# Up stage of an expert layer: slot choosing over 46 blocks, modulation with a row in PSUM, rows turned later, and 24 modulation chunks moved over from the down stage

## Chip, cores and metric

The kernel runs on one core of one Trainium2 chip. The metric is the device time of one execution in microseconds (us), lower is better. All times below are of the kernel before the change, which was executed three times for the metric and once more under the profiler.

## What is computed

Two blocks of a network follow each other on 256 tokens of width 1024. The first block ends in a layer with 16384 experts, each a row of two tables:

```python
s1 = jnp.einsum('thd,hkd->thk', q[..., :half], keys1)
s2 = jnp.einsum('thd,hkd->thk', q[..., half:], keys2)
v1, i1 = lax.top_k(s1, PEER_TOPK)
v2, i2 = lax.top_k(s2, PEER_TOPK)
...
sv, pos = lax.top_k(cand, PEER_TOPK)
eidx = jnp.take_along_axis(cidx, pos, axis=-1)
gw = jax.nn.softmax(sv, axis=-1)
...
act = jnp.einsum('td,thkd->thk', xc, u)
hact = jax.nn.gelu(act) * gc
return jnp.einsum('thk,thkd->td', hact, jnp.take(v_tab, ec, axis=0))
```

The kernel does not gather. It multiplies the tokens with all 128 x 128 rows of the table `peer_u`, takes the gelu, multiplies with a dense matrix of gates that is zero wherever an expert was not chosen, and multiplies with all of `peer_v`. The second block needs a modulation beside it: a row silu(c) of 1024 numbers times a matrix `ada_w_2` of 1024 x 6144 for each of two layers, and for two of these six parts of layer 0 a second row, silu(c of the context), as well.

## The kernel before

**The two stages.** The up stage (`u_blocks`) walks over 128 blocks of 128 experts. For one block SP (the queue of SyncE) loads 512 KB of `peer_u`; ScalarE (ACT) rounds it to a high part (`u_split`, line L1042); GpSimd (POOL) subtracts to get the low part (L1043); TensorE (PE) does 24 matmuls of 128 x 256, three products for each of eight pieces (`mm3`, L227 to L229); ACT takes the gelu into the tile A (L1055). The split of block b+2 is issued before the matmuls of block b. The down stage (`v_blocks`) walks the same way over 128 blocks of `peer_v`: ACT L1063 and VectorE (DVE) L1064 split the table, DVE L222 splits the gated activations, and PE adds up with matmuls of 128 x 512 (L308, L309, L312).

**What is laid between.** Generators give out other work, one step at a time, between the blocks (`even` shares n steps over so many blocks):

- `topk` (58 steps) chooses the experts: on DVE the maxima and their indices, then comparisons and sums that turn positions into numbers (L974 to L980), a softmax with an Exp on ACT (L983), and at the end six PE transposes (L992), copied to the PSUM tiles `picks` (L994).
- `gates` (32 steps) makes the dense gates from the picks: three DVE comparisons and products of 128 x 1024 (L1012 to L1014), eight PE matmuls of 128 x 128 into two PSUM tiles `pg` (L1019), for each of these one DVE product into A (L1021) and one ACT copy (L1023) that goes to memory (`gate_scratch`). `late_gates` reads this back in the down stage and multiplies it into the other half of A (L1033).
- `ada` (one step a chunk) makes the modulation. A chunk is 128 rows of `ada_w_2`, loaded by SP (512 KB, L171) into one of three tiles; DVE multiplies it with the row and sums along it (scalar_tensor_tensor, L180, called an STT below); a chunk with two destinations takes two. After eight chunks DVE adds the bias (L186) and `to_row` turns the result into a row: a PE transpose (L193), a DVE copy (L195) and an SP store (L196).

In the up stage `topk` runs over blocks 0 to 72, `ada0` (24 chunks, of which the first 16 have two destinations) over blocks 0 to 99, `gates` over blocks 76 to 125. In the down stage `ada1` has 72 chunks, 40 over blocks 0 to 63 and 32 over 56 blocks of the second half.

**The order.** Each engine runs its own instructions in a fixed order, which a scheduler makes from the program; an instruction waits for the ones on other engines that it needs, and everything behind it on its engine waits too. SP issues all of these loads from one queue in order.

**Memory.** The row silu(c) (`ar[:, 3]`) and the second row (`ar[:, 4]`) lie in SBUF, copied to all 128 partitions, so both inputs of an STT come from SBUF. PSUM has a pool with the tags `mm` (2 tiles), `tr` (2) and `acc` (4). `near`, `picks` and half of the `pg` tiles are `acc`.

Of the kernel before, what the change touches and what calls it, by code (L numbers as in the profile page):

```python
# [17 lines left out]
D = 1024  # L18
# [66 lines left out]
def program(tc, I, out, C, taps=None, upto=99):  # L85
# [23 lines left out]
    def ps_mm(shape=(128, 256)):  # L109
        mm_tags[1] += 1  # L110
        tag = mm_tags[0][mm_tags[1] % len(mm_tags[0])]
        return psp.tile(list(shape), F32, name=tag, bufs=4 if tag == "acc" else 2)

# [3 lines left out]
    def ps_acc(shape=(128, 512)):  # L117
        return psp.tile(list(shape), F32, name="acc", bufs=4)

# [40 lines left out]
    def ada(chunks, cs, raws, junk=None):  # L160


        todo = [(l, j, c) for l, j, _ in chunks for c in range(8)]
        got = []

        def load():
            if todo:
                l, j, c = todo.pop(0)
                raw = raws[len(got) % len(raws)]
                with tc.issue_after(last_unit[0].ins):  # L170
                    Q.dma_start(raw, I["ada_w_2"][l, (8 * j + c) * 128:(8 * j + c + 1) * 128])  # L171
                got.append(raw)

        for _ in raws:
            load()
        n = 0
# [711 lines left out]
    big = b2.enter_context(tc.tile_pool(name="big", bufs=1, reuse_waits="tile"))  # L888
    wrk.pool = b2.enter_context(tc.tile_pool(name="wrk2", bufs=2, reuse_waits="tile"))
    half0 = ExitStack()  # L890
    A = [half0.enter_context(tc.tile_pool(name="half0", bufs=1, side="right", reuse_waits="tile")), big]
# [15 lines left out]
    for c in range(16):  # L907
# [10 lines left out]
        V.tensor_copy(sc[:, :, c], pt.rearrange("p (t k) -> p t k", t=2))  # L918
    tap("sc", sc)

    wk = keep.tile([128, 2 * D], F32, name="C8")
# [4 lines left out]

    picks = []

    def topk():
        sels = [flat(b, 1).rearrange("p (s c) -> p s c", s=2) for b in (99, 103)]  # L930
        gw = flat(101, 1).rearrange("p (t h k) -> p t h k", t=2, h=8)
        near = ps_acc()
        v1 = near[:, 0:128].rearrange("p (h k) -> p h k", h=8)
# [53 lines left out]
        V.tensor_tensor(gw, gw, r8.unsqueeze(3).to_broadcast([128, 2, 8, 16]), op=OP.mult)  # L987
        picks.extend([ps_acc().rearrange("p (j t) -> p j t", j=2), ps_acc((128, T))])
        for tt in range(2):
# [8 lines left out]
    g1d = nc.dram_tensor("gate_scratch", (32, 128, 2, 256), F32, kind="Internal").ap()  # L998
    ww = itertools.cycle([("wwh", ps_tr), ("wwl", ps_acc)])

# [3 lines left out]
    def gates():  # L1004


        pick, weight = picks
        io = iota.unsqueeze(1).to_broadcast([128, 8, 128])
        for n in range(32):
            ts = slice(8 * n, 8 * n + 8)  # L1010
            oa, ob = next(oas), next(obs)
            V.tensor_tensor(oa, io, pick[:, 1, ts].unsqueeze(2).to_broadcast([128, 8, 128]), op=OP.is_equal)  # L1012
            V.tensor_tensor(ob, io, pick[:, 0, ts].unsqueeze(2).to_broadcast([128, 8, 128]), op=OP.is_equal)
            V.tensor_tensor(ob, ob, weight[:, ts].unsqueeze(2).to_broadcast([128, 8, 128]), op=OP.mult)  # L1014
            for q in range(2):
# [6 lines left out]
                st = ww_tile(name, F32R).bitcast(F32)  # L1022
# [65 lines left out]
    ut, vt = {b: u_split(b) for b in range(2)}, {}  # L1088
    ar = flat(108, 20).rearrange("p (n d) -> p n d", n=5)
    for w in range(2):  # L1090
        row(ar[:, 3 + w], f"c{w}")
    ada0 = ada([(0, j, [(j, 0)] + [(12 + j, 1)] * (j < 2)) for j in range(3)], lambda w: ar[:, 3 + w],
               [ar[:, n] for n in range(3)], flat(104, 4))
    ADA, TOPK = 24, 58

# [4 lines left out]

    tk = topk()
    for i, _ in enumerate(u_blocks(0, 76)):
        even(tk, i, TOPK, 73)
        even(ada0, i, ADA, 100)
    for _ in tk:
        pass
    g0 = gates()
    for i, _ in enumerate(u_blocks(76, 128)):
        even(g0, i, 32, 50)
        even(ada0, i + 76, ADA, 100)  # L1110
        if i + 76 == 101:
            for _ in ada0:
                pass
    for _ in g0:
        pass
# [6 lines left out]
    at = xp.tile([128, 4, D], F32, name="xdt")  # L1122
    at = [at[:, n] for n in range(4)]
    row(at[3], "c0")
    ada1 = ada([(0, j, [(j, 0)]) for j in range(3, 6)] + [(1, j, [(6 + j, 0)]) for j in range(6)], lambda w: at[3], at[:3])
# [592 lines left out]
    right.close()  # L1718
    b3.close()
    top.close()  # L1720

# [17 lines left out]
```

## Time and profile before

| what | value |
|---|---|
| median of three runs | 2160.7 us (2158.08 to 2161.99) |
| the profiled execution | 2161.18 us |
| its span in the trace | 2159.4 us |
| PE busy | 2058.1 us, 95% of the span |
| DVE busy | 1607.4 us, 74% |
| ACT busy | 1030.4 us, 48% |
| POOL busy | 795.1 us, 37% |
| moved by DMA | 403.56 MB, 187 GB/s on average |

The up stage lies between about 519 and 979 us, the down stage between there and about 1358 us. PE is busy in nearly all of the span, so a change can only save what PE loses: stretches in which it stands still, and stretches in which it runs at a lower clock. The profile gives the granted clock of a stretch as a share (1.00 is the full 2.4 GHz, and between 1.00 and 0.50 it is a mix of 2.4 and 1.2 GHz). Busy time is told for each engine apart, so the rows of a stretch must be read beside each other: which engine is full there, and for whom PE waits.

### The profile page before, as it was taken

The page shows a single profiled execution, that of the slowest core. Times are in us where ns is not written, and L with a number is a line of the kernel's source. Part 1 is how long each engine was busy: PE and PEld are TensorE (multiplying, and loading weights), DVE is VectorE, ACT ScalarE, POOL GpSimd, SP SyncE. Part 2 cuts the span into 40 slices and gives each one's busy share as a digit, 9 for nine tenths or more (in the row PEclk, how much of TensorE's full clock was granted, in tenths as well). Part 3 has the DMA queues.
Part 4 walks back from the last instruction along what each step waited for, and adds up shares of the span by engine and source line. Part 5 has one row for each costly group of instructions (what it writes and reads, how often), then busy time and mean ns, then how long its engine had stood idle before and what let it go on. Part 6 is the DMA issues. An engine that isn't in the chain of part 4 may idle for free.

```text
span 2159.4 us, 37426 instructions
## 1 busy us (share of the span) xinstructions
PE 2058.1 (95%) x14726; PEld 1898.8 (88%) x14726; DVE 1607.4 (74%) x2576; ACT 1030.4 (48%) x1732; POOL 795.1 (37%) x392
## 2 busy tenths in 40 slices
PE   8999999999879999999999999999888999899999
PEld 7989999889879999997777777899876999798998
DVE  6677688779999346758997787536785877777877
ACT  5655565454434444444444555435524545445454
POOL 2221333113957876550000000323441556343554
PEclk9999999999989999999999999999999999899999
DMA  6544544456645766559998888746224655554552
GB/s 218 159 127 135 169 128 128 133 201 200 220 138 189 231 211 189 173 174 328 349 331 318 314 280 256 166 97 76 89 69 141 194 199 181 181 171 144 193 182 98
DMA packets 122035, 403.56 MB, mean 187 GB/s; under 512 B 14561, under 2 KB 23793, under 8 KB 121858
## 3 DMA queue, kind: packets, MB, share of 16 engines
q1 hardware_dynamic: 110688, 388.43, 54.4%
q0 software_dynamic: 1520, 3.75, 2.7%
q10 hardware_dynamic: 9650, 8.99, 1.2%
q8 instruction: 115, 1.88, 0.4%
q14 instruction: 62, 0.51, 0.1%
HBM read 390.56 MB, written 10.55 MB: 186 GB/s over the span
## 4 chain that ended last, share of the span: by engine, by line
PE 68%; DVE 17%; DMA 8%; issue 3%; ACT 3%; POOL 0%; SPq 0%; DVEq 0%; ACTq 0%; POOLq 0%
PE mm L227 15%; PE mm L228 14%; PE mm L229 14%; PE acc L309 4%; PE acc L312 4%; PE acc L308 4%; DMA xdt<-in_ada_w 3%; DMA wraw<-in_peer_v 3%; DVE A L180 3%; DVE wlo L1064 3%; PE tr L1019 1%; PE acc L1019 1%; DVE wlox L222 1%; DVE wlo L222 1%; ACT whi L1063 1%
## 5 line engine op out<-in xcount | busy, mean ns | idle before, releaser
L1043 POOL TENSOR_TENSOR wlo<-wraw,whi 128x1024 fp32r<-128x1024 f32 x126 | 321.3, 2555 | 182.6 <-ACT whi L1042 182.4
L227 PE MATMUL mm<-xdt,whi 128*128 128x256 f32 x1248 | 360.7, 290 | 7.1 <-ACT A L1055 5.7
L229 PE MATMUL mm<-xdt,wlo 128*128 128x256 f32 x1248 | 355.0, 285 | 0.6 <-POOL wlo L1043 0.6
L228 PE MATMUL mm<-xdt,whi 128*128 128x256 f32 x1152 | 327.9, 285 | 0.2 <-DVE xdt L418 0.2
L1042 ACT ACTIVATE whi<-wraw 128x1024 fp32r<-128x1024 f32 x128 | 135.7, 1060 | 236.0 <-PE mm L228 152.2
L227 PEld LDWEIGHTS mm<-xdt,whi 128*128 128x128 f32 x1248 | 240.5, 193 | 8.6 <-ACT A L1055 6.3
L229 PEld LDWEIGHTS mm<-xdt,wlo 128*128 128x128 f32 x1248 | 241.0, 193 | 1.4 <-POOL wlo L1043 1.2
L228 PEld LDWEIGHTS mm<-xdt,whi 128*128 128x128 f32 x1152 | 223.1, 194 | 0.4 <-DVE xdt L418 0.4
L222 POOL TENSOR_TENSOR wlo<-wraw,whi 128x1024 fp32r<-128x1024 f32 x37 | 93.8, 2538 | 308.4 <-ACT whi L217 271.6
L1063 ACT ACTIVATE whi<-wraw 128x1024 fp32r<-128x1024 f32 x128 | 134.6, 1057 | 106.8 <-DMA wraw<-in_peer_v 100.5
L1064 DVE TENSOR_TENSOR wlo<-wraw,whi 128x1024 fp32r<-128x1024 f32 x128 | 155.5, 1220 | 23.1 <-ACT whi L1063 22.9
L222 DVE TENSOR_TENSOR wlo<-wraw,whi 128x1024 fp32r<-128x1024 f32 x87 | 134.9, 1551 | 46.7 <-ACT whi L217 46.3
L227 PE MATMUL mm<-F,whix 128*128 128x256 f32 x560 | 158.6, 284 | 7.1 <-ACT whix L217 5.0
L217 ACT ACTIVATE whi<-wraw 128x1024 fp32r<-128x1024 f32 x124 | 130.7, 1055 | 71.9 <-PE mm L228 42.4
L228 PE MATMUL mm<-F,whix 128*128 128x256 f32 x560 | 158.5, 283 | 0.4 <-DVE F L418 0.4
L229 PE MATMUL mm<-F,wlox 128*128 128x256 f32 x560 | 158.2, 283 | 0.5 <-DVE wlox L222 0.5
L309 PE MATMUL acc<-wlo,wwh 128*128 128x512 f32 x512 | 149.9, 395 | 6.6 <-DVE wlo L1064 6.4
L312 PE MATMUL acc<-whi,wwl 128*128 128x512 f32 x512 | 147.2, 394 | 5.6 <-DVE wwl L222 5.4
L308 PE MATMUL acc<-whi,wwh 128*128 128x512 f32 x512 | 141.5, 393 | 5.5 <-ACT whi L1063 5.2
L275 POOL TENSOR_TENSOR wrawx<-wrawx,grow 128x1024 f32<-128x1024 f32 x38 | 107.0, 2828 | 90.5 <-DMA wrawx<-in_ffn_w_down 47.0
L1382 POOL MEMSET att<- 128x256 f32 x4 | 1.2, 312 | 358.2 <-DVE xdt L180 358.2
L309 PEld LDWEIGHTS acc<-wlo,wwh 128*128 128x128 f32 x512 | 95.5, 189 | 32.3 <-DVE wlo L1064 12.6
(619 smaller groups left out, 6321.6 us busy)
## 6 DMA issues: line engine op xcount, KB each, us to landing
wraw<-in_peer_u SPq DMA_DIRECT2D x128, 512.0 KB
wraw<-in_peer_v SPq DMA_DIRECT2D x128, 512.0 KB
xdt<-in_ada_w SPq DMA_DIRECT2D x72, 512.0 KB
wraw<-in_ffn_w_up SPq DMA_DIRECT2D x56, 512.0 KB
wraw<-in_w_in SPq DMA_DIRECT2D x42, 512.0 KB
wrawx<-in_ffn_w_up SPq DMA_DIRECT2D x32, 512.0 KB
wrawx<-in_ffn_w_down SPq DMA_DIRECT2D x31, 512.0 KB
wrawx<-in_w_in SPq DMA_DIRECT2D x30, 512.0 KB
```

Of the source, the lines that this page charges most:

```text
L217: S.activation(hi, raw, AF.Copy)
L222: eng.tensor_tensor(lo, raw, hi.bitcast(F32), op=OP.subtract)
L227: P.matmul(ps, ah, bh, start=start, stop=False)
L228: P.matmul(ps, ah, bl, start=False, stop=False)
L229: P.matmul(ps, al, bh, start=False, stop=stop)
L308: P.matmul(acc[tt][hf], ah, hi[:, fs], start=st_, stop=False, skip_group_check=free)
L309: P.matmul(acc[tt][hf], ah, lo[:, fs], start=False, stop=False, skip_group_check=free)
L312: P.matmul(acc[tt][hf], al, hi[:, fs], start=False, stop=sp_ and not free, skip_group_check=free)
L1042: S.activation(hi, raw, AF.Copy)
L1043: (G if b in POOL_U else V).tensor_tensor(lo, raw, hi.bitcast(F32), op=OP.subtract)
L1063: last_hi[0] = S.activation(hi, raw, AF.Copy)
L1064: V.tensor_tensor(lo, raw, hi.bitcast(F32), op=OP.subtract)
```

## The change

The up stage now shares its work out in another way, and the down stage has less of it.

1. `topk` is given out over blocks 0 to 45 (before 0 to 72).
2. `ada0` comes after it: 14 chunks over blocks 46 to 63, 34 over blocks 64 to 123. It has 48 chunks in place of 24 (all of layer 0); `ada1` has 48 in place of 72, of which 18 (before 40) stand in the down stage's first half and 30 (before 32) in its second.
3. `gates` is given out over blocks 64 to 123.
4. The row silu(c) is copied into a PSUM tile `c0` of two banks by two ACT copies; `near` and `weight` get a bank each. These four banks are the ones of the `acc` tiles, whose pool is closed for the up stage and opened again after it. The second row stays in SBUF. All `pg` tiles now have the tag `tr` with two buffers.
5. `to_row` is no longer done right after the bias is added but in the middle of the next eight chunks, or at the end.
6. The chunks have three tiles of their own (`adp`) in both stages, and the program's `dynamic_dma_scratch_size` is set to 4096.

```diff
+                if c == 4:
+                    while late:
+                        slot = late.pop(0)
+                        to_row(slot, mods[:, slot])
             for slot, w in dests:
                 V.tensor_tensor(mods[:, slot], mods[:, slot], col(f"ab{l}{j}", 0, 8), op=OP.add)
-                to_row(slot, mods[:, slot])
+                late.append(slot)
+        for slot in late:
+            to_row(slot, mods[:, slot])
...
+    sums[1].close()
+    sums[1] = ExitStack()
+    sums[0] = sums[1].enter_context(tc.tile_pool(name="row", bufs=1, space=bass.MemoryType.PSUM))
+    c0 = sums[0].tile([128, D], F32, name="c0")
+    near = sums[0].tile([128, 512], F32, name="near")
+    picks = [near.rearrange("p (j t) -> p j t", j=2), sums[0].tile([128, T], F32, name="weight")]
...
-                name, pool = next(ww)
-                pg = pool((128, 512)).rearrange("p (t i) -> p t i", t=4)
+                pg = ps_tr((128, 512)).rearrange("p (t i) -> p t i", t=4)
...
+    for hf in range(2):
+        S.activation(c0[:, FS[hf]], cr[:, 0, FS[hf]], AF.Copy)
+    chunks = ([(0, j, [(j, 0)] + [(12 + j, 1)] * (j < 2)) for j in range(6)] + [(1, j, [(6 + j, 0)]) for j in range(6)])
+    raws = [adp.tile([128, D], F32, name=f"ada{n}") for n in range(3)]
+    ada0 = ada(chunks[:6], lambda w: cr[:, 1] if w else c0, raws, flat(104, 4))
...
-    for i, _ in enumerate(u_blocks(0, 76)):
-        even(tk, i, TOPK, 73)
-        even(ada0, i, ADA, 100)
...
-    for i, _ in enumerate(u_blocks(76, 128)):
-        even(g0, i, 32, 50)
-        even(ada0, i + 76, ADA, 100)
...
+    for i, _ in enumerate(u_blocks(0, 128)):
+        if i < 46:
+            even(tk, i, 58, 46)
+        elif i < 64:
+            even(ada0, i - 46, 14, 18)
+        else:
+            even(g0, i - 64, 32, 60)
+            even(ada0, i - 64, 34, 60)
...
-        even(ada1, i, 40, 64)
+        even(ada1, i, 18, 64)
...
-        even(ada1, i, 32, 56)
+        even(ada1, i, 30, 56)
```

In the changed kernel the lines have moved: L171 is L178, L180 is L187, L186 is L197, L193 is L206, L195 is L208, L196 is L209, L200 is L213, L227 to L229 are L240 to L242, L249 is L262, L974 to L980 are L991 to L997, L992 is L1008, L994 is L1010, L1012 to L1014 are L1028 to L1030, L1019 is L1034, L1043 is L1058. Three places show how the order changes.

PE before, inside u block 23: the transpose of the first modulation row (L193) stands among the block's matmuls (mm).

```order
L228 MATMUL mm<-xdt,whi 128x256
L229 MATMUL mm<-xdt,wlo 128x256
L193 MATMUL tr<-ident,mods 8x128
L227 MATMUL mm<-xdt,whi 128x256
L228 MATMUL mm<-xdt,whi 128x256
```

PE in the changed kernel, inside u block 55: the same transpose (now L206, among L240 to L242).

```order
L240 MATMUL mm<-xdt,whi 128x256
L241 MATMUL mm<-xdt,whi 128x256
L206 MATMUL tr<-ident,mods 8x128
L242 MATMUL mm<-xdt,wlo 128x256
L240 MATMUL mm<-xdt,whi 128x256
```

The transpose has moved back by 32 u blocks.

DVE before, around the bias of the first row (L186): the STTs (L180) stand between the steps of the choosing (L974, L978, L980).

```order
L974 TENSOR_TENSOR A_5787<-acc,iota 128x1024
L180 SCALAR_TENSOR_TENSOR A_5787,mods<-A_5787 128x1024
L980 TENSOR_REDUCE A_5787<-A_5787 128x64
L978 TENSOR_TENSOR A_5787<-A_5787,acc 128x1024
L180 SCALAR_TENSOR_TENSOR A_5787,mods<-A_5787 128x1024
L186 TENSOR_TENSOR mods<-mods,cols 128x8
```

DVE in the changed kernel, from the last step of the choosing on (`near` and `weight` are PSUM tiles, c_6370 the row in PSUM, ada_ the chunk's tile, A_5793 a scratch tile and, as an input of a chunk's second STT, the second row).

```order
L997 TENSOR_REDUCE A_5793<-A_5793 128x64
L1010 COPY near<-tr 128x2x128 x2
L1028 TENSOR_TENSOR C_6373<-iota,near 128x1024
L1029 TENSOR_TENSOR C_6373<-iota,near 128x1024
L1028 TENSOR_TENSOR oa<-iota,near 128x1024
L1029 TENSOR_TENSOR ob<-iota,near 128x1024
L1030 TENSOR_TENSOR C_6373<-C_6373,weight 128x1024
L1030 TENSOR_TENSOR ob<-ob,weight 128x1024
L187 SCALAR_TENSOR_TENSOR A_5793,mods<-ada_6394,c_6370 128x1024
L187 SCALAR_TENSOR_TENSOR ada_6394,mods<-ada_6394,A_5793 128x1024
L187 SCALAR_TENSOR_TENSOR A_5793,mods<-ada_6395,c_6370 128x1024
L187 SCALAR_TENSOR_TENSOR ada_6395,mods<-ada_6395,A_5793 128x1024
```

All STTs now stand behind the choosing and behind the first gates' comparisons.

SP before, the loads of `peer_u` and of the chunks:

```order
L249 DMA wraw<-in_peer_u 128x1024 x7
L171 DMA A_5787<-in_ada_w 128x1024 x3
L249 DMA wraw<-in_peer_u 128x1024 x2
L171 DMA A_5787<-in_ada_w 128x1024
L249 DMA wraw<-in_peer_u 128x1024 x2
L171 DMA A_5787<-in_ada_w 128x1024
L249 DMA wraw<-in_peer_u 128x1024 x4
```

and in the changed kernel (row_c is the second row, read into its tile):

```order
L262 DMA wraw<-in_peer_u 128x1024 x6
L213 DMA A_5793<-row_c 128x1024
L262 DMA wraw<-in_peer_u 128x1024 x44
L178 DMA ada_6394<-in_ada_w 128x1024
L178 DMA ada_6395<-in_ada_w 128x1024
L178 DMA ada_6396<-in_ada_w 128x1024
L262 DMA wraw<-in_peer_u 128x1024 x2
L178 DMA ada_6394<-in_ada_w 128x1024
L262 DMA wraw<-in_peer_u 128x1024
L178 DMA ada_6395<-in_ada_w 128x1024
L178 DMA ada_6396<-in_ada_w 128x1024
```

The first three chunks have moved from behind the 7th load of `peer_u` to behind the 50th, and from there on chunks and `peer_u` loads take turns nearly one to one.

## Rows read from the trace of the kernel before

**Rows 1.** Windows: us, busy of PE, PEld, DVE, ACT, POOL, clock, DMA share, GB/s

```profile
518.00:979.00 461.00, 436.16 (x3605) 432.90 (x3604) 329.13 (x545) 198.60 (x329) 321.32 (x126) 0.97 0.60 194
...
700.00:800.00 100.00, 100.00 (x842) 100.00 (x841) 43.18 (x47) 45.84 (x76) 77.79 (x32) 1.00 0.68 223
```

**Rows 2.** Waits of PE in the up stage: total us, times, longest

```profile
PE tr L193 <- DVE mods L186: 18.1, 1, 18.1
PE mm L227 <- ACT A L1055: 5.7, 3, 4.3
PE mm L229 <- POOL wlo L1043: 0.6, 3, 0.2
```

**Rows 3.** Windows of 20 us around the two longest waits

```profile
580.00:600.00 20.00, 8.23 (x69) 8.02 (x67) 20.00 (x40) 5.32 (x8) 12.17 (x5) 0.78 0.53 176
600.00:620.00 20.00, 13.64 (x96) 13.66 (x97) 19.59 (x43) 4.00 (x6) 6.84 (x3) 0.71 0.21 58
...
640.00:660.00 20.00, 15.67 (x111) 15.47 (x110) 19.73 (x35) 9.00 (x12) 12.46 (x5) 0.83 0.56 180
```

**Rows 4.** Timeline of PE at the end of the longest wait

```profile
606.36 0.37 PE L193 MATMUL tr<-ident,mods 128*8 128x128 f32 x1 [18.13 <-DVE mods L186]
```

**Rows 5.** Timeline of DVE there

```profile
606.05 0.16 DVE L186 TENSOR_TENSOR mods<-mods,cols 128x8 f32<-128x8 f32 x1
```

**Rows 6.** Line L180, up stage: duration ns min/median/max, first and last start

```profile
L180 DVE SCALAR_TENSOR_TENSOR A<-A x40: 1201/2579/3422, 529.6 to 813.6; 128x1024 f32<-128x1024 f32 x40
```

**Rows 7.** Timeline of POOL, before and after the STTs' dense stretch

```profile
547.72 18.73 POOL L1043 TENSOR_TENSOR wlo<-wraw,whi 128x1024 fp32r<-128x1024 f32 x6 [0.36 <-ACT whi L1042]
...
569.10 2.40 POOL L1043 TENSOR_TENSOR wlo<-wraw,whi 128x1024 fp32r<-128x1024 f32 x1 [0.28 <-ACT whi L1042]
```

**Rows 8.** Timeline of ACT: two gelus a block apart, then the Exp

```profile
641.80 0.37 ACT L1055 ACTIVATE A<-mm 128x256 f32<-128x256 f32 x1
...
644.68 0.37 ACT L1055 ACTIVATE A<-mm 128x256 f32<-128x256 f32 x1
645.06 1.28 ACT L983 ACT_TABLE_LOAD   x1
650.72 0.42 ACT L983 ACTIVATE A<-A 128x256 f32<-128x256 f32 x1 [4.37 <-DVE A L982]
```

**Rows 9.** Window of DVE's choosing, all lines

```profile
474.00:679.00 205.00, 180.16 (x1454) 178.36 (x1453) 199.48 (x527) 82.16 (x122) 121.38 (x45) 0.93 0.57 186
```

**Rows 10.** The same window, line L180 alone (DVE busy)

```profile
474.00:679.00 205.00, 64.54 (x52) 0.93 0.57 186
```

**Rows 11.** Groups by line, 500 to 1000 us: DVE products with a PSUM input

```profile
L1014 DVE TENSOR_TENSOR ob<-ob,acc 128x1024 f32<-128x1024 f32 x16 | 19.5, 1218 | 0.4
...
L1021 DVE TENSOR_TENSOR A<-A,acc 128x256 f32<-128x256 f32 x32 | 13.5, 420 | 32.5 <-PE acc L1019 32.5
...
L1023 ACT ACTIVATE wwl<-acc 128x256 f32<-128x256 f32 x32 | 12.3, 384 | 12.1 <-DVE A L1021 12.1
```

**Rows 12.** Windows of the down stage

```profile
1020.00:1120.00 100.00, 92.65 (x395) 72.72 (x394) 96.74 (x134) 45.73 (x67) 0.00 (x0) 1.00 0.94 340
1120.00:1160.00 40.00, 40.00 (x179) 32.91 (x178) 34.35 (x53) 21.00 (x30) 0.00 (x0) 1.00 0.87 313
1170.00:1360.00 190.00, 183.64 (x804) 147.01 (x804) 145.55 (x224) 98.83 (x147) 2.18 (x9) 1.00 0.85 286
```

**Rows 13.** DVE groups by line, 1020 to 1120 us

```profile
L1064 DVE TENSOR_TENSOR wlo<-wraw,whi 128x1024 fp32r<-128x1024 f32 x33 | 40.0, 1218 | 3.2 <-ACT whi L1063 3.2
L180 DVE SCALAR_TENSOR_TENSOR xdt<-xdt 128x1024 f32<-128x1024 f32 x21 | 25.5, 1215 | 0.0
...
L1033 DVE TENSOR_TENSOR A<-A,ob 128x512 f32<-128x512 f32 x12 | 13.1, 1090 | 0.0
```

**Rows 14.** Waits of PE, 980 to 1170 us

```profile
PE acc L309 <- DVE wlo L1064: 6.2, 8, 1.4
```

**Rows 15.** Waits of SP's queue, 500 to 1000 us

```profile
SPq L249 <- POOL wlo L1043: 354.8, 123, 5.9
```

More of the change, by code (lines that the diff above doesn't have):

```diff
@@ L96, in program, with open_sums @@
     psp = top.enter_context(tc.tile_pool(name="psp", bufs=2, space=bass.MemoryType.PSUM))
+    sums = [None, None]
+    def open_sums():
+        sums[1] = ExitStack()
+        sums[0] = sums[1].enter_context(tc.tile_pool(name="sums", bufs=4, space=bass.MemoryType.PSUM))
+    open_sums()
     stream = top.enter_context(tc.tile_pool(name="stream", bufs=3, reuse_waits="tile"))
@@ L111, in ps_mm @@
         tag = mm_tags[0][mm_tags[1] % len(mm_tags[0])]
-        return psp.tile(list(shape), F32, name=tag, bufs=4 if tag == "acc" else 2)
+        return ps_acc(shape) if tag == "acc" else psp.tile(list(shape), F32, name=tag, bufs=2)
     def ps_tr(shape):
@@ L117, in ps_acc @@
     def ps_acc(shape=(128, 512)):
-        return psp.tile(list(shape), F32, name="acc", bufs=4)
+        return sums[0].tile(list(shape), F32, name="acc")
     x0 = I["x"].rearrange("b (n p) d -> p (b n) d", p=128)
@@ L175, in ada @@
             load()
-        n = 0
+        n, late = 0, []
         for l, j, dests in chunks:
@@ L889, in program @@
     wrk.pool = b2.enter_context(tc.tile_pool(name="wrk2", bufs=2, reuse_waits="tile"))
+    adp = b2.enter_context(tc.tile_pool(name="adp", bufs=1, reuse_waits="tile"))
     half0 = ExitStack()
@@ L919, in program @@
     tap("sc", sc)
+    sums[1].close()
+    sums[1] = ExitStack()
+    sums[0] = sums[1].enter_context(tc.tile_pool(name="row", bufs=1, space=bass.MemoryType.PSUM))
+    c0 = sums[0].tile([128, D], F32, name="c0")
+    near = sums[0].tile([128, 512], F32, name="near")
+    picks = [near.rearrange("p (j t) -> p j t", j=2), sums[0].tile([128, T], F32, name="weight")]
     wk = keep.tile([128, 2 * D], F32, name="C8")
@@ L925, in program @@
     G.dma_start(iota, C["iota"])
-    picks = []
     def topk():
@@ L931, in topk @@
         gw = flat(101, 1).rearrange("p (t h k) -> p t h k", t=2, h=8)
-        near = ps_acc()
         v1 = near[:, 0:128].rearrange("p (h k) -> p h k", h=8)
@@ L987, in topk @@
         V.tensor_tensor(gw, gw, r8.unsqueeze(3).to_broadcast([128, 2, 8, 16]), op=OP.mult)
-        picks.extend([ps_acc().rearrange("p (j t) -> p j t", j=2), ps_acc((128, T))])
         for tt in range(2):
@@ L998, in program @@
     g1d = nc.dram_tensor("gate_scratch", (32, 128, 2, 256), F32, kind="Internal").ap()
-    ww = itertools.cycle([("wwh", ps_tr), ("wwl", ps_acc)])
+    ww = itertools.cycle(("wwh", "wwl"))
     def ww_tile(name, dt):
@@ L1021, in gates @@
                 V.tensor_tensor(dst, dst, pg[:, :, 0:64].rearrange("p t b -> p b t"), op=OP.mult)
-                st = ww_tile(name, F32R).bitcast(F32)
+                st = ww_tile(next(ww), F32R).bitcast(F32)
                 S.activation(st.rearrange("p (t b) -> p t b", t=4), pg[:, :, 64:128], AF.Copy)
@@ L1088, in program @@
     ut, vt = {b: u_split(b) for b in range(2)}, {}
-    ar = flat(108, 20).rearrange("p (n d) -> p n d", n=5)
+    cr = flat(108, 8).rearrange("p (w d) -> p w d", w=2)
     for w in range(2):
[L1091 to L1094, printed above, removed]
+        row(cr[:, w], f"c{w}")
+    for hf in range(2):
[3 more added lines that the diff above has]
+    ada0 = ada(chunks[:6], lambda w: cr[:, 1] if w else c0, raws, flat(104, 4))
     def even(gen, i, n, blocks):
@@ L1099, in even @@
             next(gen, None)
-    tk = topk()
-    for i, _ in enumerate(u_blocks(0, 76)):
-        even(tk, i, TOPK, 73)
-        even(ada0, i, ADA, 100)
-    for _ in tk:
-        pass
-    g0 = gates()
-    for i, _ in enumerate(u_blocks(76, 128)):
-        even(g0, i, 32, 50)
-        even(ada0, i + 76, ADA, 100)
[L1111 to L1115, printed above, removed]
+    tk, g0 = topk(), gates()
+    for i, _ in enumerate(u_blocks(0, 128)):
[6 more added lines that the diff above has]
+            even(ada0, i - 64, 34, 60)
+    for g in (g0, ada0):
+        for _ in g:
+            pass
+    sums[1].close()
+    open_sums()
     xx = [unit(x1d[tt]) for tt in range(2)]
@@ L1121, in program @@
             P.matmul(acc[tt][hf], ident, xx[tt][:, hf * 512:hf * 512 + 512], start=True, stop=True)
[L1122 to L1125, printed above, removed]
+    cr0 = xp.tile([128, 4, D], F32, name="xdt")[:, 3]
+    row(cr0, "c0")
+    ada1 = ada(chunks[6:], lambda w: cr0, raws)
     g1 = late_gates()
@@ L1719, in program @@
     b3.close()
+    sums[1].close()
     top.close()
@@ L1726 @@
     from concourse.bass_utils import run_bass_kernel_spmd
-    nc = bacc.Bacc("TRN2", target_bir_lowering=False, num_devices=1)
+    nc = bacc.Bacc("TRN2", target_bir_lowering=False, num_devices=1, dynamic_dma_scratch_size=4096)
     arrays, I, C = {}, {}, {}
```

## The prediction

> **What bounds the kernel now.** I read the windows first: they tell where PE loses time at all. In the up stage PE is busy 436.16 of 461.00 us [rows 1], so it stands still for 24.8 us; from 700 to 800 us it loses nothing [rows 1], and the reader is to see that the loss lies in the first third. The view of waits says for whom PE stood: 18.1 us once for the bias of the first modulation row (DVE L186), 5.7 us in three waits for a gelu, of which one is 4.3, and 0.6 us for POOL's split [rows 2]. Together that is 24.4 of the 24.8. To this comes the clock: 13.64 us of work were done at a granted clock of 0.71 in the 20 us in which the long wait ended, 15.67 us at 0.83 in the 20 us around the 4.3 us wait [rows 3]. At full clock these would have taken 13.64 x 0.29 = 4.0 and 15.67 x 0.17 = 2.7 us less. The up stage loses 24.8 + 4.0 + 2.7 = **31.5 us** in all.
>
> The two timelines say why. PE's transpose of the row waited 18.13 us [rows 4] for the bias that DVE did at 606.05 [rows 5], while DVE was busy for all of 580 to 600 us [rows 3]: not idle, but too full. From 474 to 679 us DVE is busy 199.48 us [rows 9], of which 64.54 are STTs [rows 10], so choosing itself is some 135 us. An STT takes 1.2 us at best, 2.58 in the median, 3.42 at worst [rows 6]; POOL's split takes 2.40 us alone and 18.73 / 6 = 3.12 us with an STT beside it [rows 7]. DVE and POOL hold each other up, and a block of PE lasts only 2.88 us (the distance of two gelus) [rows 8]. The 4.3 us wait is one of order as well: ACT stood at the Exp until 650.72 us, 4.37 us for DVE, with the gelu behind it [rows 8].
>
> In the down stage the window from 1020 to 1120 us has 395 matmuls in 100 us, with DVE 96.74 busy; in the next 40 us, in which DVE is busy 34.35, it is 179, or 447 in 100 [rows 12]. PE waits there for DVE's split above all: 6.2 us in eight waits [rows 14]. DVE's list for these 100 us holds 25.5 us of STTs and 13.1 us of late gates in one of their two buffers [rows 13]. So this half is bound by DVE, with DMA not far off (0.94 of its time, 340 GB/s [rows 12]).
>
> **The change, part by part.** (1) *Choosing over 46 blocks, no STT among it, row turned late.* The transposes of rows 0 and 12 move from u blocks 23 and 24 to 55 and 56; the Exp moves from behind gelu 36 to behind gelu 26. What made DVE late, 40 STTs in the middle of choosing, is gone from there, so the 18.1 and 4.3 us waits and the 6.7 us of slow clock go. What is late next: PE's first transposes of the chosen slots, now within blocks 16 and 18. Adding up DVE's own durations in its new order, what the first needs is done after 83 of the 135 us, so at about 474 + 83 = 557 us, and 562 with two short operations held up for some 2 us by POOL; PE reaches block 16 at 518 + 16 x 2.88 = 564. The margin is about 2 us, for block 18 the same; later ones have 10. I take 0.5 us for this and 0.5 us for the Exp, whose table load of 1.28 us [rows 8] stands before a gelu; bounds 0 and the 18 us of the old wait.
>
> (2) *The 16 double chunks, now in blocks 46 to 66.* One STT of each reads the row from PSUM, the other both inputs from SBUF. Products with a PSUM input take 1.22 us while POOL works [rows 11], so the first one is free of this; the second is not. Per chunk that is one collision, about as in the old dense stretch. There, about ten splits at 3.12 us cost PE only the 0.6 us for POOL and the two shorter waits for gelus, 5.7 - 4.3 = 1.4 us [rows 2], since the split runs ahead of PE. Lower bound: 2.0 x 16 / 10 = 3 us. Upper bound: no overlap at all, 2.40 [rows 7] + 1.20 [rows 6] = 3.60 us a block, 16 x (3.60 - 2.88) = 11.5 us. I take 6, nearer to the lower bound, since that row shows the same pair.
>
> The Trainium skill's page "SBUF — State Buffer", section "SBUF: two separate sides", has a rule that speaks against this: VectorE and GpSimd share a port pair as an exclusive lock for a whole instruction, also for a VectorE operation with two SBUF inputs. By that rule the pair would cost the upper bound; the trace's 3.12 us [rows 7] is less than 3.60, so I don't take it in full.
>
> (3) *24 more chunks in the up stage, single, in blocks 64 to 123.* Each is one STT of 1.22 us from PSUM [rows 11]. DVE is busy 43 of 100 us from 700 on [rows 1], and the whole of them is 24 x 1.22 = 29 us, spread over 170 us: hidden by the matmuls. Their loads, 24 x 0.52 = 12.6 MB, add some 70 GB/s to the 194 [rows 1], under the 340 that the down stage shows [rows 12]. SP is moved past them one for one: a load of `peer_u` now stands behind a chunk's, which waits until DVE has read the tile three chunks back. SP's queue waits for POOL's split in nearly all of its loads anyway, 354.8 us [rows 15], so I cost this at nothing; without that cover it costs what rival A costs.
>
> (4) *Gates from block 64, `pg` in two buffers.* The work is the same. A gate comes every other block and uses the buffers of the gate before, some 5 us after it; DVE's product and ACT's copy take 0.42 and 0.38 us [rows 11]. Nothing, unless DVE is late (rival D).
>
> (5) *The down stage's first half with 18 chunks in place of 40.* 22 STTs at 1.22 us give DVE 27 us in 64 blocks, 12 or so of it in the 100 us window. Bounds: it then goes at the pace of the second half, 804 matmuls in 190 us or 423 in 100 [rows 12], a gain of 100 x (1 - 395 / 423) = 6.6 us; or at the pace of the 40 us without late gates, 447, a gain of 100 x (1 - 395 / 447) = 11.6. I take 9, the middle. The second half loses two chunks: nothing. (6) *The copies of the row to PSUM, two on ACT,* and the smaller DMA scratch: under 1 us, hidden by ACT's idle half of the stage (198.60 of 461 busy [rows 1]).
>
> **Sum.** 31.5 - 6 - 1 = 24.5 in the up stage, 9 in the down stage: 33.5 us. The profiled execution took 2161.2 us, half a microsecond above the median of 2160.7: 2161.2 - 33.5 = **2128 us**, and 2122 to 2136 with the bounds of (2) and (5).
>
> **Rivals.**
> *A, the dense stretch is bound by DVE.* If the PSUM product doesn't fit beside POOL's split, a chunk takes 1.22 + 2.58 = 3.80 us [rows 6, 11], PE loses 16 x 0.92 = 14.7 us in place of 6, and the transpose in block 55 is late again by some 4 us, with 3 us of slow clock: 2128 + 8.7 + 7 = 2144. For it: old STTs filled DVE. Against it: DVE had choosing beside them.
> *B, the down stage gives nothing back*, because DMA (0.94 [rows 12]) takes DVE's place: 2128 + 9 = 2137. Against it: the 40 us at full pace have 0.87.
> *C, the change doesn't do what it says:* choosing is late at blocks 16 and 18, so that the wait only moves; the old wait's 18 us come back in place of 0.5: 2146.
> *D, slower.* With two `pg` buffers PE waits at each of 64 groups for DVE's product, which stands behind a stretched STT, and for ACT's copy. At the 0.42 + 0.38 us of the two [rows 11] 64 groups cost 51 us: 2179. It decides from 33.5 / 64 = 0.5 us a group. Against it: PE runs through 700 to 800 us, gates included, without a loss [rows 1], and gates come less densely now.
> *E, a split and an STT with both inputs in SBUF never overlap.* Then the upper bound of (2) holds: 2128 + 5.5 = 2134. For it: a median STT of 2.58 us [rows 6] has waited for more than its own 1.2. Against it: 3.12 us for both [rows 7].
>
> **How the numbers follow.** Forecast 0.46, A 0.15, E 0.13, B 0.12, C 0.07, D 0.05, and 0.02 for a loss that vanishes nearly whole, 31.5 + 11.6 = 43 us or 2118. About 0.2% (4 us) is what a measurement of this kernel can tell from no change. Only D ends slower: 0.05. A, B and C come singly at 2137 to 2146, all faster; two or three of them together reach the bound at 2156, for which I set 0.04 as no difference; 0.91 is left for faster. The range takes in A, B, C and E singly and 3 us below 2118: 2115 to 2147. It leaves out D, sums of rivals, and some of the tails of A and C.
>
> **What would show it.** Right: no wait of PE for L197's bias over 2 us, granted clock 1.00 from 580 to 660 us, PE waits for POOL and gelus of together 4 to 8 us between 650 and 710, over 420 matmuls in 100 us after 1020 (33 us earlier). Wrong: a long wait of PE for a transpose in blocks 16, 18 or 55, for the product of L1036 or for `pg`, or a down stage with DMA at 0.95 and the old pace.

## The result, and the profile after the change

The changed kernel takes 2122.9 us in the median of four runs (2118.3 to 2128.9), beside 2159.4 us of the kernel before: a ratio of 0.9834 with a 95% interval of 0.9801 to 0.9867. Forecast were 2128 us and 2115 to 2147. The profiled execution is the fastest of the four, 2118.32 us, 42.9 us under the profiled one of before; by the medians it is 36.5 us, so the two profiles show the change at its best. Where these 42.9 us came from is read by stages, from the first gelu to the first matmul with the gated activations, from there to the 257th of the 512 such matmuls on L308 (L321 in the changed kernel), to the last one, and to the end:

| stage (us) | before | after | difference |
|---|---|---|---|
| up | 456.2 | 433.0 | -23.2 |
| down, first half | 193.8 | 179.4 | -14.4 |
| down, second half | 185.2 | 181.9 | -3.3 |
| everything behind | 801.0 | 797.8 | -3.2 |

The first gelu comes 1.3 us later than before. A second profile of the changed kernel, from a later batch, has 437.9, 182.0, 181.8 and 793.9 us in these four rows. In the twelve experiments below the part behind the down stage took 793.9 to 803.6 us, so the last row tells nothing of the change.

The waits of PE in the changed kernel from 480 to 1000 us (us in all, times, longest; the first line lies behind the up stage, in the down stage):

```profile
PE acc L322 <- DVE wlo L1079: 3.0, 2, 1.9
PE tr L206 <- DVE mods L197: 1.5, 1, 1.5
PE tr L1034 <- ACT wwh L1038: 1.5, 1, 1.5
PE mm L242 <- POOL wlo L1058: 1.1, 4, 0.5
PE mm L240 <- ACT A L1070: 0.8, 1, 0.8
PE tr L1008 <- DVE A L1004: 0.7, 1, 0.7
```

The 18.1 us for the bias and the 5.7 us for gelus [rows 2] have shrunk to 1.5 and 0.8 (1.5 and 1.6 in the second profile). Windows of the same kernel (columns as in [rows 1]):

```profile
600.00:620.00 20.00, 19.28 (x160) 18.90 (x159) 18.31 (x17) 9.50 (x17) 15.79 (x7) 1.00 0.55 178
620.00:640.00 20.00, 20.00 (x169) 20.00 (x168) 3.99 (x4) 9.16 (x15) 16.59 (x7) 1.00 0.58 184
...
660.00:680.00 20.00, 19.32 (x158) 18.77 (x157) 19.79 (x25) 8.66 (x13) 17.55 (x7) 1.00 0.85 305
680.00:700.00 20.00, 18.53 (x157) 18.34 (x156) 19.93 (x28) 8.27 (x12) 16.93 (x7) 1.00 0.85 297
700.00:720.00 20.00, 17.88 (x141) 16.87 (x139) 19.86 (x25) 7.09 (x12) 17.30 (x6) 1.00 0.83 286
720.00:740.00 20.00, 19.37 (x163) 19.37 (x164) 8.95 (x16) 8.71 (x15) 14.28 (x6) 1.00 0.78 269
740.00:760.00 20.00, 20.00 (x173) 20.00 (x172) 17.99 (x24) 10.55 (x19) 14.28 (x6) 1.00 0.70 243
```

PE now loses its time where DVE is full with double chunks (660 to 720 us), the clock stays at 1.00, and from 740 us on nothing is lost, gates and 24 more chunks included. From 620 to 640 us DVE has hardly anything to do: the choosing is over and the first chunk is not there yet. The timeline of DVE shows a double chunk, two STTs, in its steady state, and that of POOL the splits beside it:

```profile
665.75 1.21 DVE L187 SCALAR_TENSOR_TENSOR A<-ada,c 128x1024 f32<-128x1024 f32 x1
...
667.00 2.17 DVE L187 SCALAR_TENSOR_TENSOR ada<-ada,A 128x1024 f32<-128x1024 f32 x1
...
669.10 1.21 DVE L187 SCALAR_TENSOR_TENSOR A<-ada,c 128x1024 f32<-128x1024 f32 x1
```

```profile
661.75 9.68 POOL L1058 TENSOR_TENSOR wlo<-wraw,whi 128x1024 fp32r<-128x1024 f32 x3 [0.38 <-ACT whi L1057]
```

The STT that reads the row from PSUM (c) takes its 1.21 us while POOL is splitting; the one with both inputs in SBUF takes 2.17. One chunk follows the other after 3.35 us. In the down stage the stretch that answers to [rows 12] reads

```profile
998.00:1098.00 100.00, 99.70 (x440) 81.77 (x441) 88.25 (x120) 51.27 (x73) 0.00 (x0) 1.00 0.87 299
1098.00:1138.00 40.00, 40.00 (x178) 33.14 (x177) 29.79 (x41) 21.98 (x30) 0.00 (x0) 1.00 0.80 277
```

that is 440 matmuls in 100 us, nearly the pace of the 40 us behind it, with DVE 88 busy in place of 97.

### The profile page after: what moved, and what is told of

Its sections match the earlier page's. It is cut to its first block, busy times and chain, and to the rows that moved or that the text cites. A ratio compares the mean times of both kernels' runs of the same rounds, so it can differ in the third digit from the quotient of the medians.

```text
span 2116.6 us, 37474 instructions
## 1 busy us (share of the span) xinstructions
PE 2052.5 (97%) x14726; PEld 1900.0 (90%) x14726; DVE 1562.8 (74%) x2576; ACT 1033.7 (49%) x1734; POOL 782.3 (37%) x392
## 4 chain that ended last, share of the span: by engine, by line
PE 76%; DVE 12%; DMA 5%; issue 3%; ACT 2%; POOL 0%; SPq 0%; ACTq 0%; DVEq 0%; POOLq 0%
PE mm L240 16%; PE mm L241 16%; PE mm L242 15%; PE acc L322 6%; PE acc L325 6%; PE acc L321 5%; DMA ada<-in_ada_w 3%; PE tr L1034 3%; DVE ada L187 2%; DVE wlo L1079 2%; DMA wraw<-in_peer_v 1%; DVE A L187 1%; DVE wlox L235 1%; PE acc L240 1%; PE acc L241 1%
## 5 line engine op out<-in xcount | busy, mean ns | idle before, releaser
L1058 POOL TENSOR_TENSOR wlo<-wraw,whi 128x1024 fp32r<-128x1024 f32 x126 | 312.8, 2490 | 172.2 <-ACT whi L1057 171.0
L240 PE MATMUL mm<-xdt,whi 128*128 128x256 f32 x1248 | 357.2, 287 | 2.3 <-DVE xdt L470 1.1
L242 PE MATMUL mm<-xdt,wlo 128*128 128x256 f32 x1248 | 353.5, 284 | 1.2 <-POOL wlo L1058 1.1
L240 PEld LDWEIGHTS mm<-xdt,whi 128*128 128x128 f32 x1248 | 238.3, 192 | 3.7 <-DVE xdt L470 1.6
L242 PEld LDWEIGHTS mm<-xdt,wlo 128*128 128x128 f32 x1248 | 238.9, 191 | 2.3 <-POOL wlo L1058 2.2
L235 POOL TENSOR_TENSOR wlo<-wraw,whi 128x1024 fp32r<-128x1024 f32 x37 | 92.9, 2512 | 308.8 <-ACT whi L230 272.0
L240 PE MATMUL mm<-F,whix 128*128 128x256 f32 x560 | 158.4, 283 | 5.3 <-ACT whix L230 4.2
L242 PE MATMUL mm<-F,wlox 128*128 128x256 f32 x560 | 158.2, 283 | 0.8 <-DVE wlox L235 0.8
L322 PE MATMUL acc<-wlo,wwh 128*128 128x512 f32 x512 | 143.1, 391 | 4.4 <-DVE wlo L1079 4.4
L325 PE MATMUL acc<-whi,wwl 128*128 128x512 f32 x512 | 141.3, 391 | 2.5 <-DVE wwl L235 2.4
L321 PE MATMUL acc<-whi,wwh 128*128 128x512 f32 x512 | 139.8, 391 | 0.2 <-ACT whi L1078 0.2
```

Source lines behind the costliest of these rows:

```text
L235: eng.tensor_tensor(lo, raw, hi.bitcast(F32), op=OP.subtract)
L240: P.matmul(ps, ah, bh, start=start, stop=False)
L242: P.matmul(ps, al, bh, start=False, stop=stop)
L321: P.matmul(acc[tt][hf], ah, hi[:, fs], start=st_, stop=False, skip_group_check=free)
L322: P.matmul(acc[tt][hf], ah, lo[:, fs], start=False, stop=False, skip_group_check=free)
L325: P.matmul(acc[tt][hf], al, hi[:, fs], start=False, stop=sp_ and not free, skip_group_check=free)
```

## The experiments

My theory: choosing without STTs among it and the row in PSUM together took PE's waits for DVE away; the late turn of the rows carries nothing, and the down stage gained DVE time. The rivals are that one part alone carries the up stage, and that the down stage gained DMA time. Each edit is against the changed kernel unless it says otherwise; "before" is the kernel before, timed beside them.

**The rows turned at once.**

```diff
-                late.append(slot)
+                to_row(slot, mods[:, slot])
```

> The changed kernel with the rows turned right after their bias again (one line). My theory: the late turn carries nothing, because the schedule puts the transposes of rows 0 and 12 at the same places of PE's order with it or without (u blocks 55 and 56); what took the 18 us wait away is that choosing is done before the modulation begins. Expected 2123 us, within 4, and one wait of PE for the bias of under 3 us. Rival, the late turn is what took the wait away: 2141 to 2148, with a wait for the bias of 15 us or more.

Measured: 2122.8 us, ratio 0.9823 (0.9797 to 0.9849). The late turn is worth nothing: the two transposes stand at the same places of PE's order with it and without. The wait of PE for the first bias was 3.6 us in the profiled execution:

```profile
PE tr L206 <- DVE mods L197: 3.6, 1, 3.6
```

and the up stage 437.5 us, with the clock at 0.91 in the 20 us of that wait. The changed kernel's own second profile has 437.9, so 433.0 is its good case. The 3.6 us are not the early turn's either: the two runs below that edit the down stage alone, with the late turn in place, have the same 3.6 us, and up stages of 440.7 and 436.1 us.

**Only the late turn**, in the kernel before (the same lines of `ada` as in the change).

> The kernel before with nothing but the late turn of the rows in the program. My theory: the schedule puts the transposes of rows 0 and 12 where they were, so the 18 us wait stays: 2156 to 2163. Rival, the late turn alone removes the wait: 2130 to 2142.

Measured: 2161.5 us, ratio 0.9994 (0.9976 to 1.0011), and the old wait as it was:

```profile
PE tr L199 <- DVE mods L190: 18.1, 1, 18.1
PE mm L233 <- ACT A L1061: 5.8, 3, 4.3
```

**Both rows from SBUF.** (The tile of the row lies in the storage of A's last blocks, so the last chunks are multiplied with gelus there in place of the row; the amount of work is the same.)

```diff
-    for hf in range(2):
-        S.activation(c0[:, FS[hf]], cr[:, 0, FS[hf]], AF.Copy)
...
-    ada0 = ada(chunks[:6], lambda w: cr[:, 1] if w else c0, raws, flat(104, 4))
+    ada0 = ada(chunks[:6], lambda w: cr[:, w], raws, flat(104, 4))
```

> The changed kernel with both rows read from SBUF (no copy to PSUM). My theory: each STT now collides with a POOL split, so a double chunk takes two splits, some 6.3 us in place of 3.35; the first eight chunks end about 24 us later, and PE's transpose in block 55 waits for most of that, 15 to 24 us, with slow clock behind it: 2138 to 2155 us. Rival, the row in PSUM matters little because DVE has idle time around the stretch: 2123 to 2128.

Measured: 2150.3 us, ratio 0.9941 (0.9922 to 0.9960), up stage 463.9 us, longer than before the change. Timeline of DVE, one double chunk:

```profile
660.57 3.41 DVE L187 SCALAR_TENSOR_TENSOR A<-ada,A 128x1024 f32<-128x1024 f32 x1
663.92 0.08 DVE L187 DVE_READ_ACCUMULATOR A<-ada,A 128x1 f32 x1
664.03 3.30 DVE L187 SCALAR_TENSOR_TENSOR ada<-ada,A 128x1024 f32<-128x1024 f32 x1
```

Each STT waits out a split, 6.7 us a chunk. The wait for the bias is only part of the loss; PE waits longer for the gates' PSUM buffers and for gelus:

```profile
PE tr L1034 <- ACT wwh L1038: 8.7, 3, 5.0
PE tr L206 <- DVE mods L197: 6.1, 1, 6.1
PE mm L240 <- ACT A L1070: 6.0, 3, 5.3
PE mm L242 <- POOL wlo L1058: 3.1, 3, 1.4
```

Once PE stands still POOL has no split to do, and the STTs from 670.72 to 676.70 us take 1.22 us again; I take this for the reason why the wait for the bias was 6 us and not the 15 to 24 that I expected of it, though the total came out as expected. A part of the loss may be the experiment's own: late in the stage a gelu waits for an STT that reads the storage it is to write, and PE then loses 4.1 us from 920 to 960 us.

```profile
ACT A L1070 <- DVE ada L187: 2.0, 1, 2.0
```

```profile
920.00:940.00 20.00, 17.58 (x145) 16.97 (x143) 19.97 (x20) 6.19 (x11) 12.34 (x4) 1.00 0.76 253
940.00:960.00 20.00, 18.32 (x142) 18.32 (x143) 18.76 (x23) 10.12 (x18) 13.96 (x6) 0.91 0.60 200
```

**The 24 chunks back in the down stage.**

```diff
-    ada0 = ada(chunks[:6], lambda w: cr[:, 1] if w else c0, raws, flat(104, 4))
+    ada0 = ada(chunks[:3], lambda w: cr[:, 1] if w else c0, raws, flat(104, 4))
...
-            even(ada0, i - 64, 34, 60)
+            even(ada0, i - 64, 10, 60)
...
-    ada1 = ada(chunks[6:], lambda w: cr0, raws)
+    ada1 = ada(chunks[3:], lambda w: cr0, raws)
...
-        even(ada1, i, 18, 64)
+        even(ada1, i, 40, 64)
...
-        even(ada1, i, 30, 56)
+        even(ada1, i, 32, 56)
```

> The changed kernel with the 24 chunks back in the down stage (40 in the first half, 32 after). My theory: the first half of the down stage is bound by DVE again and gives back the 14 us that it had gained, while the up stage stays as in the changed kernel: 2132 to 2140 us. Rival, the down stage gained by its new order at the start or its own chunk tiles: 2121 to 2127. Rival, the 24 chunks cost the up stage as much as they save below: same time as the changed kernel, with a shorter up stage.

Measured: 2143.7 us, ratio 0.9908 (0.9887 to 0.9929): 21 us above the changed kernel, more than expected; 17.7 of them show in the down stage, as 14.8 and 2.9 us over the first profile (15.2, as 12.2 and 3.0, over the second), the others in the up stage and behind. The first half of the down stage is back at 194.2 us, the second at 184.8; the up stage took 440.2 us. The window of the first half, from its first matmul on:

```profile
965.00:1159.00 194.00, 181.30 (x774) 144.03 (x773) 176.45 (x254) 88.02 (x126) 0.00 (x0) 0.99 0.92 334
```

Kernels with the changed kernel's down stage take between 179.4 and 184.4 us for this half in eight profiles. So the moved chunks were worth 10 to 15 us in it, and they cost the up stage nothing: without them it took 440.2 us, with them 433.0 to 440.7.

**The order alone**: both rows from SBUF, rows turned at once and the chunks back, by the edits above (the last chunks are multiplied with gelus here too, but PE loses nothing there).

> The changed kernel with three parts undone: rows from SBUF, rows turned at once, 24 chunks back. What stays is choosing over 46 blocks with modulation behind it and the gates' two buffers. My theory: the old wait at block 23 goes (about 29 us with the 4.3 us wait and the clock), and most of that comes back as a wait in block 55, since double chunks take 6.3 us: 2148 to 2163 us. Rival, the order alone carries the up stage's gain of 22 us: 2134 to 2141.

Measured: 2158.3 us, ratio 0.9989 (0.9972 to 1.0006). The up stage takes 452.9 us, 3.3 less than before the change: the old wait is gone and comes back between 660 and 740 us as waits for gelus, splits and the bias:

```profile
PE mm L240 <- ACT A L1070: 6.7, 4, 4.3
PE mm L242 <- POOL wlo L1058: 4.9, 4, 2.4
PE tr L206 <- DVE mods L197: 4.1, 2, 3.6
```

**The row in PSUM with the old order.**

```diff
-        if i < 46:
-            even(tk, i, 58, 46)
-        elif i < 64:
-            even(ada0, i - 46, 14, 18)
-        else:
-            even(g0, i - 64, 32, 60)
-            even(ada0, i - 64, 34, 60)
+        if i < 73:
+            even(tk, i, 58, 73)
+        if i < 124:
+            even(ada0, i, 48, 124)
+        if i >= 76:
+            even(g0, i - 76, 32, 50)
```

> The changed kernel with its steps shared out as before: choosing over 73 blocks with modulation (48 chunks over 124 blocks, row in PSUM) among it from the start, gates from block 76. My theory: the order is needed too, since the row in PSUM shortens a double chunk to 3.35 us but DVE is full with choosing anyway: a wait of PE for the first row's bias, now asked for in block 14, of 15 to 30 us, total 2138 to 2155. Rival, the row in PSUM alone carries the up stage's gain: 2120 to 2128.

Measured: 2132.4 us, ratio 0.9866 (0.9835 to 0.9897), between my range and the rival's, nearer to the rival. The up stage takes 441.7 us. The wait for the biases falls to 5.6 us although the first is asked for in block 14, and the Exp's wait stays:

```profile
PE tr L206 <- DVE mods L197: 5.6, 3, 2.9
PE mm L240 <- ACT A L1070: 5.2, 1, 5.2
```

I had DVE later than it was. The second STT takes less than in the dense stretch, 1.76 us in the median in place of 2.17; I put this down to the choosing that stands between two collisions, which no run tested:

```profile
L187 DVE SCALAR_TENSOR_TENSOR ada<-ada,A x16: 1195/1761/3129, 532.0 to 628.0; 128x1024 f32<-128x1024 f32 x16
```

**Loads without products in the down stage's first half.** The spare tiles are read by nobody.

```diff
+    def more_loads():
+        for n in range(22):
+            with tc.issue_after(last_unit[0].ins):
+                Q.dma_start(spare[:, n % 3], I["ada_w_2"][1, (24 + n) * 128:(25 + n) * 128])
+            yield
...
         even(ada1, i, 18, 64)
+        even(extra, i, 22, 64)
```

> The changed kernel with 22 more loads of 512 KB in the first half of the down stage that nobody reads, so that as many bytes move there as before, without their products. My theory: that half was bound by DVE, so loads alone cost little: the half grows from 179 us by 0 to 4 us, total 2121 to 2127. Rival, the transfers were what bound it (0.94 of the DMA time before): the half goes back to 190 to 194 us, total 2132 to 2138.

**Products without loads**, at the same place.

```diff
+            V.scalar_tensor_tensor(spare[:, n % 2], cr0, 1.0, cr0, op0=OP.mult, op1=OP.mult,
+                                   accum_out=spare[:, 2, n:n + 1])
```

> The changed kernel with 22 more STTs of 128 x 1024 in the first half of the down stage, over a row that lies in SBUF already, so that DVE has the work of before without the loads. My theory: the half grows from 179 us by 9 to 14 us, total 2131 to 2138. Rival (transfers bound it): 0 to 4 us, total 2121 to 2127.

Measured: the loads 2129.5 us, ratio 0.9865 (0.9842 to 0.9888), first half 182.9 us; the products 2146.7 us, ratio 0.9942 (0.9926 to 0.9958), first half 206.4 us. Both totals are above what I expected, and the sizes of the half are what decides. The windows of that half, first with the loads, then with the products:

```profile
964.00:1147.00 183.00, 177.91 (x774) 143.75 (x773) 152.84 (x203) 90.03 (x128) 0.00 (x0) 1.00 0.95 351
```

```profile
959.00:1166.00 207.00, 186.92 (x775) 143.68 (x774) 176.10 (x248) 90.69 (x128) 0.00 (x0) 0.98 0.76 259
```

With the DMA busy 0.95 of the time, more than before the change, PE stands still for 5.1 us in this half; with the DMA at 0.76 and DVE loaded it is 20 us, at a lower clock. DVE is what bound it: 182.9 us lies inside the 179.4 to 184.4 of kernels without these loads. Two things don't fit to the microsecond. The products cost more than the 10 to 15 us of the chunks themselves: nothing holds them back, and the schedule put all 22 into the first 73 us,

```profile
L1144 DVE SCALAR_TENSOR_TENSOR xdt<-xdt x22: 1210/1225/1232, 963.7 to 1036.7; 128x1024 f32<-128x1024 f32 x22
```

so that they are paid early in the half, where I take DVE to have had the least to spare. And the loads' total is 8 us above the changed kernel's of the same batch, of which the half shows 0.9 (182.9 beside 182.0); the rest lies in other stages, 2.8 us of it in the up stage, which the edit doesn't touch, and I leave it open.

**The modulation begun earlier.**

```diff
-        elif i < 64:
-            even(ada0, i - 46, 14, 18)
-        else:
+        if 36 <= i < 64:
+            even(ada0, i - 36, 14, 28)
+        if i >= 64:
```

> The changed kernel with the first 14 modulation steps shared out over blocks 36 to 63 in place of 46 to 63; DVE does next to nothing between choosing (612 us) and the first chunk (656 us). My theory: PE's loss between 660 and 720 us (7 to 12 us over the runs so far) comes from the density, one double chunk of 3.35 us per block of 2.88 us; spread out, POOL catches up between two collisions and the loss falls to 2 to 4 us: 2113 to 2119. Rival, each collision costs PE a fixed part whatever the density: same time as the changed kernel. Rival, the transposes of the rows, which move with it to blocks 47 and 48, wait as long there: same time.

**The changed kernel again**, in the same batch.

> The changed kernel itself beside the three others: 2118 to 2128 us as before, with PE's wait for the first row's bias at 1.5 to 4 us and the first half of the down stage at 179 to 181 us.

Measured: 2121.3 us, ratio 0.9832 (0.9804 to 0.9860), and 2121.5 us, ratio 0.9829 (0.9797 to 0.9861): no difference, where I had expected 2113 to 2119 of the earlier start. The transpose of the row moves along with the modulation and waits where it now stands:

```profile
PE tr L206 <- DVE mods L197: 2.8, 1, 2.8
PE mm L242 <- POOL wlo L1058: 1.1, 4, 0.4
```

So the second rival fits: the wait for a gate's buffer is gone, the splits' part is 1.1 us beside 1.1 and 2.9 in the two profiles of the changed kernel, and the wait for the bias, 2.8 us beside 1.5, is most of the 3.9 us that PE stands still from 620 to 680 us.

**The rows really turned late**, by an order behind the newest block's matmuls.

```diff
-            P.transpose(pt, src, ident)
+            with ExitStack() as st:
+                if last_mm[0] is not None and behind[0]:
+                    st.enter_context(tc.issue_after(last_mm[0].ins))
+                P.transpose(pt, src, ident)
...
-        P.matmul(ps, al, bh, start=False, stop=stop)
-
+        last_mm[0] = P.matmul(ps, al, bh, start=False, stop=stop)
...
```

> The changed kernel with the transposes of the rows ordered behind the newest u block's matmuls at the point where the program asks for them, so that the late turn really happens: rows 0 and 12 are transposed in u block 64 in place of 55 and 56. My theory: the wait for the bias (1.5 to 3.6 us) and the slow clock behind it go, up stage 430 to 433 us in place of 433 to 438, total 2115 to 2120. Rival: PE then reaches the splits and the gates that much earlier and waits for POOL or ACT in place of the bias; same time as the changed kernel, 2120 to 2124.

**The same with the modulation begun earlier.**

> The same, with the first 14 modulation steps shared out over blocks 36 to 63. My theory: of the loss of 8 to 13 us in the up stage only the Exp and the chosen slots' transposes (1.5 us) and 1 to 2 us for POOL are left: up stage 427 to 430 us, total 2111 to 2117. Rival, the time of the up stage is bound elsewhere as well (gates, the first down blocks): 2118 to 2124.

Measured: alone 2125.8 us, ratio 0.9832 (0.9805 to 0.9859); with the earlier start 2119.5 us, ratio 0.9803 (0.9776 to 0.9829). Both are above what I expected; the second lies where its rival put it. Alone it does nothing: the transposes now stand right ahead of the first gates and share their PSUM buffers, so that PE waits there for DVE's copy of the row, 4.0 us. With the earlier start nearly every wait of the up stage is gone,

```profile
PE tr L1014 <- DVE A L1010: 0.7, 1, 0.7
PE mm L247 <- POOL wlo L1064: 0.6, 3, 0.2
PE mm L245 <- ACT A L1076: 0.6, 2, 0.3
PE tr L1040 <- DVE row L213: 0.3, 1, 0.3
```

and the up stage takes 430.2 us, the shortest seen and at the end of the 427 to 430 that I expected. In the total that is 2 to 3 us by the medians and some 6 by the ratios, whose intervals overlap: it may beat the changed kernel, which these runs don't settle.

## Why the prediction was right, and where it was not

*The up stage's sum.* Forecast 24.5 us; the profiled executions of the changed kernel give 23.2 and 18.3 (456.2 less 433.0 and 437.9), and the two runs that edit the down stage alone 15.5 and 20.1. So the size is about right, and high in all four. A part of that is the clock's 4.0 us for 600 to 620 us: the 0.71 belongs to a window in which PE stood still until 606.36. The window has 96 matmuls in 13.64 us [rows 3], where a full one has 169 in 20 us (620 to 640 us above); at that pace 96 take 11.4 us, so 2.3 us were lost and not 4.0. The view that carried the sum was that of the waits. The clock stayed at 1.00 from 580 to 660 us as forecast.

*Which part brings it.* My step (1) gave the whole gain to the order, and (2) counted the rest as a price. That is the step that was wrong, though the time came out: the order alone brings 3.3 us, the row in PSUM with the old order 14.5 (456.2 less 441.7), both together 15.5 to 23.2 in the four profiles. The two singly add up to 17.8, inside this spread, so the runs don't show that one needs the other. With the new order the row in PSUM is worth 12.7 us: that is 452.9 with the order alone less 440.2 with the 24 chunks back, two kernels that differ in it and in the turn of the rows, which is worth nothing. So the row in PSUM carries most of the up stage's gain under either order. The order takes the STTs out of choosing, but without the PSUM row most of the loss only moves to 660 to 740 us. Of the part "row turned late" nothing was left: the schedule puts the transposes where it pleases. I listed it in (1) without asking what it does alone.

*The dense stretch (2).* Forecast 6 us between bounds of 3 and 11.5. One chunk follows every 3.35 us. The 3.12 that I read from [rows 7] is a mean over six splits, of which the last ran after the STTs had ended; single splits of that trace take 3.38 us beside an STT and 2.4 without one:

```profile
543.97 3.38 POOL L1043 TENSOR_TENSOR wlo<-wraw,whi 128x1024 fp32r<-128x1024 f32 x1
...
564.04 4.77 POOL L1043 TENSOR_TENSOR wlo<-wraw,whi 128x1024 fp32r<-128x1024 f32 x2
```

So the pair cost the same before the change as after it, nearer to rival E's 3.60 than I took it, and rival A's 3.80 did not come. The "SBUF — State Buffer" page of the Trainium skill ("SBUF: two separate sides") has the shared port pair as an exclusive lock; the pair of a split and an STT is 0.25 us shorter than the two alone, so by these spans a small part of the two overlaps. The same page of the Trainium skill ("Who interferes with whom") has an instruction with at most one SBUF input stay out of it, which agrees with the 1.21 us of the first STT. PE's loss from 660 to 720 us, idle time of the windows above, is 0.68 + 1.47 + 2.12 = 4.3 us in the first profile. Up to 740 us it is 4.9 us there and 7.5 us in the second profile, with the clock at 0.91 in the last 20 us of that. So the size holds, but not the make-up: I had named waits for POOL and gelus of 4 to 8 us between 650 and 710 us, and they are 0.7 us in the first profile and 3.1 in the second; the bias (1.5 us, and 3.6 in four other runs with this stretch) and a gate's buffer (1.5) make up most of the rest. The wait for the bias I had put into rival A alone; it belongs in the forecast, and my limit of 2 us for it holds in both profiles of the changed kernel only.

*The choosing's own margin.* No wait at blocks 16 and 18; 0.7 us for a later transpose and 0.8 for a gelu at the Exp, 1.5 us in place of my 1.0. Rival C did not come.

*24 more chunks, and two buffers for the gates (3, 4).* Nothing lost after 740 us, one wait of 1.5 us for a buffer. Rival D did not come; but the SBUF experiment shows its mechanism at 8.7 us when DVE is late, with ACT's copies (L1038) waiting for DVE's products (L1036), so the condition that I gave it was the right one.

*The down stage (5).* 9 us were forecast; the first profile has 14.4, the second 11.8, and all eight profiles with this down stage lie between 9.4 and 14.4. So the term was small by up to 5 us. I priced 100 us of the half. The 40 us ahead of them gained as well, 146 matmuls before and 162 in the first profile (159 in the second); the windows of the one and of the other:

```profile
980.00:1020.00 40.00, 36.12 (x146) 27.75 (x145) 36.61 (x53) 15.65 (x24) 0.00 (x0) 0.96 0.93 342
```

```profile
958.00:998.00 40.00, 37.02 (x162) 29.68 (x160) 36.28 (x49) 18.52 (x27) 0.00 (x0) 1.00 0.95 344
```

That DVE and not DMA bound the half was right, so rival B did not come. The second half's 3.3 us I had at nothing; it comes back with the 24 chunks (184.8), but also with the loads alone (186.0) and with both rows in SBUF (184.8), whose edits leave this half alone. Its cause was not looked for.

*The total.* It came out closer than its terms: the up stage gave 1 to 9 us less than forecast, the first half of the down stage 0.4 to 5.4 us more, and the second half some 3 us that were not in the sum. That these nearly cancel is luck.

## What to carry to other kernels

A wait of one engine for another tells where the loss shows, not which work to move: sum the work of the engine that is waited for over the whole stretch, and ask what each part of a change does alone. One profile of a kernel is one draw: here the same stage differed by 5 to 8 us between profiles, as much as some of the terms. When two engines hold each other up over SBUF, moving one input to PSUM can be worth more than another order, as here with 13 to 15 us beside the 3 of the order alone. A line that asks for something later changes nothing where a scheduler sets the order; look at the order, and tie it down if it must move.

## What the runs showed of the hardware that was not expected

Very small products wait as long as large ones; I had allowed some 2 us for two of them, and here it is that much for one. The bias of 128 x 8 numbers takes 0.16 us alone [rows 5]; at the end of the dense stretch two of them took 2.43 us in all, and two scalings of the same size 2.41. Of each pair the first took 2.36 and 2.33 us, the second 0.15:

```profile
712.60 2.43 DVE L197 TENSOR_TENSOR mods<-mods,cols 128x8 f32<-128x8 f32 x2
714.99 2.41 DVE L1148 SCALAR_TENSOR_TENSOR msc<-mods,cols 128x8 f32<-128x8 f32 x2
```

```profile
698.70 18.61 POOL L1058 TENSOR_TENSOR wlo<-wraw,whi 128x1024 fp32r<-128x1024 f32 x6 [0.52 <-ACT whi L1057]
```

POOL was splitting without a break from 698.70 for 18.61 us then, and each of the two long ones ended within 0.03 us of a split's end. Alone the four would have cost 0.6 us; the rest is the wait for a split.
